# A hybrid encoder trunk on one core: modulations as products in column quarters, and written orders for the first stage and the units

## The chip, the cores and the metric

The kernel runs on one core of one Trainium2 chip. The core has a matrix engine (TensorE, PE in the rows; its weight loads are PEld), three engines for elementwise work (VectorE or DVE, ScalarE or ACT, GpSimd or POOL), and SyncE (SP), which here only issues transfers. Each engine runs its own list of instructions in order and waits on semaphores for the others. The metric is the device time of one execution in microseconds; lower is better.

## The reference, cut to what matters

Two residual layers of width 1024 over 512 tokens; layer 0 mixes by S5 and attention, layer 1 by a gated linear recurrence, each followed by an MLP with a squared ReLU. Shift, scale and gate of every part come from a conditioning vector `c`.

```python
mod = (c_act @ ada_w[layer] + ada_b[layer])            # 1024 x 6144
sh1, sc1, g1, sh2, sc2, g2 = jnp.split(mod, 6, axis=-1)
u = rms_norm(h, norm_w[layer, 0]) * (1.0 + sc1) + sh1
z = u @ hyb_w_in[e]                                     # columns: s5 | q | k | v
# s5, for each of two directions: abar = exp(lr*dt) * (cos, sin)(li*dt); b scaled by f(abar);
# complex linear scan over the 512 tokens; y += Re(h c); then gelu and a gated linear unit
# attention: rms norm of each head of q and k, rotary tables, softmax(q k / 8) v
mix = jnp.concatenate([y_s5, y_att], axis=-1) @ hyb_w_out[e]
h = h + g1 * mix
```

All is float32; the kernel multiplies large matrices as three products of rounded parts (`wh`, `wl` the rounded weight and its remainder; `acta`, `actb` the same of the activations).

## The kernel before

Only `hybrid` (L1113 to L1242), the first part of layer 0, is touched. It has four stretches.

*First stage.* x is loaded as eight tiles `h` of 128 features by 512 tokens. `rstd_bc` (L742) adds their squares (ACT squares into `nt`, DVE adds into `nacc`, L752) and spreads the reciprocal root. The modulation of features comes in four blocks of 512 columns (256 of shift, 256 of scale), each for two tiles: `ada_load` fetches the eight raw tiles of a block, `ada_block` (L708) adds them up on DVE, weighted by a column of `cact` (L715 a multiply, L717 seven multiply-adds of 128x512), and four products with `ones` (L719) fold the partitions. `norm_tile` then makes `acta` (ACT, L769) and `actb` (DVE, L770) of one tile, `wtile` casts its weights (`wh` on ACT, L512; `wl`, the remainder, L513, on POOL for the first three tiles and on DVE after), and TensorE adds 36 products for k and v (`psk`, 256 columns) and q (`psq`, 512), L599 to L601.

*Parameters.* `s5_params` (L164) makes the powers of abar, some hundred operations on 32 to 160 columns. It runs on POOL; the class `Tiny` splits the forms that POOL does in two. `s5_tables` (L290) makes sine tables on DVE and ACT. `s5_prep` (L328) forms the scaled b and c of one unit (`s5par` is fetched on ACT's queue; complex products `s5vr`, `s5vi`, `s5cv`, L341 to L345, on POOL but for one unit; ACT copies them to `s5c`, L356, and `s5bx`), transposes them, and `s5_lag` multiplies the lags on TensorE (L406) into `s5dc` on DVE (L415, L421).

*To the first unit.* `s5_in` makes the s5 columns of z in two halves (8 tiles each). `attn_kv` and `attn_q`: `head_ss` (L899) squares each head of 64 columns with an accumulator; q is rotated (`qr`), multiplied by its reciprocal root on POOL (L945), cast on ACT (L946) and the cast subtracted on POOL (L947).

*Units.* Eight units, for four groups in two directions (`for i in range(8)`). A unit makes phases (`s5_phase`, ACT), its states (`s5_states`: products L441 into `pb` and `p`, DVE multiplies L446 to L448, four scans L455 into `actb`), and the turn back (`s5_turn`: four POOL multiplies L466 to L469, two DVE additions L472 and L473, products L477). Beside them run attention steps (`step`): scores L967 and L968, maximum on DVE L970, exponential on ACT L972, transposes L980, products with v L989. `STEPS` gives their count before and after the next preparation: 23 of 35 calls in the units, the rest in `fill`. Gate (0, 2) is made by `ada_half`: 16 transfers on ACT's queue and 16 DVE operations (L668, L673), half of them each at the units in `FIN`.

A scheduler with its own costs sets each engine's order; the written code sets only the order on equal terms and the buffers. Behind the units come `fill` (the gated unit, the output products) and the boundary norm, then the MLP, layer 1 and its MLP.

Of the kernel before, what the change touches and what calls it, by code (L numbers as in the profile page):

```python
# [19 lines left out]
P = 128  # L20
# [5 lines left out]
STEPS = ((2, 2),) * 5 + ((2, 1),) + ((0, 0),) * 2  # L26
PREP_V = (2,)

EARLY, FIN = (0, 0, 2), (3, 4)
# [31 lines left out]


class Tiny:


    def __init__(self, kern, pool, eng):
        self.kern, self.pool, self.eng = kern, pool, eng
        self.tensor_scalar, self.tensor_tensor = eng.tensor_scalar, eng.tensor_tensor
        self.tensor_copy, self.memset = eng.tensor_copy, eng.memset

    def scalar_tensor_tensor(self, out, a, s, b, op0, op1):
        n = math.prod(out.shape[1:])
        t = self.kern.tl(self.pool, "tiny", [P, 160], bufs=2)[:, 0:n]
        if len(out.shape) == 3:
            t = t.rearrange("p (a b) -> p a b", b=out.shape[2])
        self.eng.tensor_scalar(t, a, s, None, op0=op0)  # L76
        self.eng.tensor_tensor(out, t, b, op=op1)


class Kern:  # L80
# [54 lines left out]
    def setup(self, cols, consts):  # L135
# [23 lines left out]
        self.sel = self.cp.tile([P, 32], F32, tag="sel", name="sel")  # L159
        self.glubh = self.cp.tile([P, 4], F32, tag="glubh", name="glubh")  # L160
# [3 lines left out]
    def s5_params(self, sp, tp):  # L164
        nc = self.nc
        V = D = Tiny(self, tp, nc.gpsimd)
# [6 lines left out]
        def pexp(x):  # L173
            n, r, p, o = t("n"), t("r"), t("p"), self.tl(tp, self.nm("pexp"), [P, W])
            V.tensor_scalar(n, x, 1.4426950408889634, MAGIC, op0=ALU.mult, op1=ALU.add)
            V.tensor_scalar(n, n, MAGIC, None, op0=ALU.subtract)
            V.scalar_tensor_tensor(r, n, -0.693359375, x, op0=ALU.mult, op1=ALU.add)
            V.scalar_tensor_tensor(r, n, 2.12194440e-4, r, op0=ALU.mult, op1=ALU.add)
            V.tensor_scalar(p, r, 1.9875691500e-4, None, op0=ALU.mult)
            for cf in (1.3981999507e-3, 8.3334519073e-3, 4.1665795894e-2, 1.6666665459e-1, 5.0000001201e-1, 1.0):  # L180
                V.scalar_tensor_tensor(p, p, cf, r, op0=ALU.add, op1=ALU.mult)
            V.tensor_scalar(p, p, 1.0, None, op0=ALU.add)
            V.tensor_scalar(n, n, -127.0, 128.0, op0=ALU.max, op1=ALU.min)
            e = t("e", dt=I32)
            V.tensor_scalar(e, n, 127.0, 8388608.0, op0=ALU.add, op1=ALU.mult)
            V.tensor_tensor(o, p, e.bitcast(F32), op=ALU.mult)
            return o
# [3 lines left out]
        dt = pexp(ldt)  # L191
# [11 lines left out]
        def reduce(a, n):  # L203

            D.tensor_scalar(n, a, 0.15915494309189535, MAGIC, op0=ALU.mult, op1=ALU.add)
            D.tensor_scalar(n, n, MAGIC, None, op0=ALU.subtract)
            for c in (c1, c2, c3):
                D.scalar_tensor_tensor(a, n, -c, a, op0=ALU.mult, op1=ALU.add)
            D.tensor_scalar(a, a, -pi, pi, op0=ALU.max, op1=ALU.min)

        def sincos(co, si, a, n):
            reduce(a, n)
            nc.vector.scalar_tensor_tensor(n, a, -1.0, a, op0=ALU.mult, op1=ALU.min)
            D.tensor_scalar(n, n, math.pi / 2, None, op0=ALU.add)
            nc.scalar.activation(si, a, AF.Sin)
            nc.scalar.activation(co, n, AF.Sin)

        reduce(r, t("rn"))
# [6 lines left out]
        for lo, ks in ((0, slice(0, 5)), (16, slice(4, None, -1))):  # L225
            D.tensor_tensor(ppi[:, lo:lo + 16], r[:, lo:lo + 16].unsqueeze(2).to_broadcast([P, 16, 5]),
                            kidx[:, ks].unsqueeze(1).to_broadcast([P, 16, 5]), op=ALU.mult)
        sincos(pr, ppi, ppi, npr)
        mag = pexp(x)
        V.memset(mt, 1.0)  # L230
        m = lambda k: ((mt[:, 0:16, k], slice(0, 16)), (mt[:, 16:32, 4 - k], slice(16, 32)))
        for o, h in m(1):
            nc.scalar.copy(o, mag[:, h])
        m2 = t("m2")
        V.tensor_tensor(m2, mag, mag, op=ALU.mult)
        for o, h in m(2):
            nc.scalar.copy(o, m2[:, h])
        for o, h in m(3):
            V.tensor_tensor(o, m2[:, h], mag[:, h], op=ALU.mult)
# [14 lines left out]
        nr, den, ta, fr, fi = t("nr"), t("den"), t("ta"), t("fr"), t("fi")  # L254
        V.tensor_scalar(nr, ar, 1.0, None, op0=ALU.subtract)
        V.tensor_tensor(den, lr, lr, op=ALU.mult)
        V.tensor_tensor(ta, li, li, op=ALU.mult)
        V.tensor_tensor(den, den, ta, op=ALU.add)
        nc.vector.reciprocal(den, den)
        V.tensor_tensor(fr, nr, lr, op=ALU.mult)  # L260
        V.tensor_tensor(ta, ai, li, op=ALU.mult)
        V.tensor_tensor(fr, fr, ta, op=ALU.add)
        V.tensor_tensor(fr, fr, den, op=ALU.mult)
        V.tensor_tensor(fi, ai, lr, op=ALU.mult)
        V.tensor_tensor(ta, nr, li, op=ALU.mult)
        V.tensor_tensor(fi, fi, ta, op=ALU.subtract)
# [5 lines left out]
        tb = self.tl(tp, "s5tb", [P, W, 4])  # L272
        for lo in (0, 16):
            sl = slice(lo, lo + 16)
            sv = slice(3, None, -1) if lo == 0 else slice(4, 0, -1)

            def b4(x):
                return x[:, sl].unsqueeze(2).to_broadcast([P, 16, 4])

            V.tensor_tensor(fpr[:, sl], pr[:, sl, sv], b4(fr), op=ALU.mult)  # L280
            V.tensor_tensor(tb[:, sl], npi[:, sl, sv], b4(fi), op=ALU.mult)
            V.tensor_tensor(fpr[:, sl], fpr[:, sl], tb[:, sl], op=ALU.add)
            V.tensor_tensor(fpi[:, sl], pr[:, sl, sv], b4(fi), op=ALU.mult)
            V.tensor_tensor(tb[:, sl], ppi[:, sl, sv], b4(fr), op=ALU.mult)
            V.tensor_tensor(fpi[:, sl], fpi[:, sl], tb[:, sl], op=ALU.add)
        nc.scalar.mul(nfpi, fpi, -1.0)
        V.tensor_scalar(r, r, 0.15915494309189535, None, op0=ALU.mult)
        self.s5 = dict(pr=pr, npr=npr, npi=npi, fpr=fpr, fpi=fpi, nfpi=nfpi, m4=m4, turns=r)

# [38 lines left out]
    def s5_prep(self, tp, pg, d, bc_dram, eng):  # L328

        nc, s5 = self.nc, self.s5  # L330
# [4 lines left out]
        nc.scalar.dma_start(par, bc_dram[d * 4 + pg].rearrange("p (a x c) -> p a x c", a=4, x=4))  # L335
# [17 lines left out]
        for src, dst in zip(cv, cs):  # L353
            for g in range(2):
                r = slice(g * 64, g * 64 + 64)
                A.copy(dst[r, :, g], src[r])  # L356

# [7 lines left out]
        sl0 = 3 if d == 0 else 0  # L365
        bx = []
        for j, src in enumerate((vr, vi)):
            t = self.tl(tp, f"s5bx{j}", [P, 4, 4, 16], bufs=1)
            A.copy(t, src[:, :, sl0].unsqueeze(2).to_broadcast([P, 4, 4, 16]))
            bx.append(t)  # L370
        self.s5u[(pg, d)] = bt, cs
        return bx, cs

    def s5_phase(self, sp, pg, d, eng):

# [1288 lines left out]
```

## Time and profile before

| | us |
|---|---|
| median of 3 runs (lowest to highest) | 1255.64 (1254.99 to 1257.53) |
| profiled execution, its own time | 1256.23 |
| its span, first to last instruction | 1254.4 |
| TensorE busy (share of the span) | 1161.8 (93%) |
| DVE busy | 804.5 (64%) |
| ACT busy | 532.3 (42%) |
| POOL busy | 240.4 (19%) |
| mean granted clock of TensorE | 0.959 |

Times in the rows are us from the start of the span; 1.8 us of the profiled execution's time lie outside it. Matmuls overlap in the rows, so a sum of their durations is more than the time they take. A float32 product (not rounded) shows as two records. A wait is put down to the releaser that came last.

### The profile page before, as it was taken

To read this page: it belongs to the slowest core of one execution; us is meant where nothing else is said; L and a number is where in the kernel's file an instruction comes from. 1 tells how busy PE (TensorE), PEld (TensorE's weight loads), DVE (VectorE), ACT (ScalarE), POOL (GpSimd) and SP (SyncE) were. 2 spreads that over 40 slices of the span, in tenths; PEclk is the share of its full clock that TensorE was granted. 3 is DMA by queue.
4 is the path that set the end of the run, shared out by engine and by line. 5 is a ranking of instruction groups with operands and counts; after the bars stand their busy time and mean duration, and the time that the engine had idled before them with its cause. 6 is when DMAs were issued, how large, how long until landed. Compare 5 with 4: busy or idle time off the path is not lost.

```text
span 1254.4 us, 16894 instructions
## 1 busy us (share of the span) xinstructions
PE 1161.8 (93%) x6456; PEld 983.0 (78%) x6456; DVE 804.5 (64%) x1182; ACT 532.3 (42%) x962; POOL 240.4 (19%) x346
## 2 busy tenths in 40 slices
PE   3678798889999999999999999789999999999997
PEld 2568577667998888888888988569988888888887
DVE  7548897988789875678433789995753332445243
ACT  3147577645452332134322449853543321334130
POOL 9996995410000000000000053000000000000000
PEclk9989697979999999999999999789999999999998
DMA  9411301065538765667332332112242223322311
GB/s 337 130 56 58 113 20 35 2 201 153 194 108 272 265 205 190 208 204 248 102 101 85 101 109 76 51 56 79 73 129 88 98 101 101 90 96 101 101 34 67
DMA packets 83856, 151.74 MB, mean 121 GB/s; under 512 B 5696, under 2 KB 30272, under 8 KB 83776
## 3 DMA queue, kind: packets, MB, share of 16 engines
q1 hardware_dynamic: 75712, 137.04, 33.6%
q10 hardware_dynamic: 8064, 13.64, 3.5%
q8 instruction: 50, 0.82, 0.3%
q14 instruction: 30, 0.25, 0.1%
HBM read 148.55 MB, written 2.10 MB: 120 GB/s over the span
## 4 chain that ended last, share of the span: by engine, by line
PE 71%; DVE 13%; POOL 8%; ACT 3%; issue 2%; DMA 1%; SPq 0%; ACTq 0%; DVEq 0%; POOLq 0%
PE ps L560 13%; PE ps L561 12%; PE ps L559 12%; PE px L559 8%; PE px L561 8%; PE px L560 8%; DVE wl L513 2%; POOL tiny L76 1%; DVE actb L455 1%; DMA wr<-wout 1%; PE py L477 1%; PE po L989 1%; DVE ti L1411 1%; DVE hs L1410 1%; DVE esum L970 1%
## 5 line engine op out<-in xcount | busy, mean ns | idle before, releaser
L513 DVE TENSOR_TENSOR wl<-wr,wh 128x1024 fp32r<-128x1024 f32 (+2 forms) x175 | 211.3, 1208 | 298.4 <-ACT wh L512 291.5
L512 ACT CAST wh<-wr 128x1024 fp32r<-128x1024 f32 (+2 forms) x170 | 173.6, 1022 | 436.5 <-PE ps L560 200.1
L560 PE MATMUL ps<-actb,wh 128*128 128x512 f32 (+1 forms) x512 | 181.3, 354 | 0.1
L559 PE MATMUL ps<-acta,wh 128*128 128x512 f32 (+1 forms) x328 | 116.8, 357 | 0.0
L561 PE MATMUL ps<-acta,wl 128*128 128x512 f32 (+1 forms) x328 | 116.1, 355 | 0.0
L559 PE MATMUL ps<-hid,wh 128*128 128x512 f32 x288 | 112.1, 389 | 0.0
L561 PE MATMUL ps<-hid,wl 128*128 128x512 f32 x288 | 112.0, 389 | 0.0
L560 PE MATMUL ps<-hid,wh 128*128 128x512 f32 x288 | 112.0, 389 | 0.0
L560 PEld LDWEIGHTS ps<-actb,wh 128*128 128x128 f32 x512 | 97.7, 191 | 13.5 <-DVE actb L849 0.3
L559 PE MATMUL px<-hid,wh 128*128 128x512 f32 (+1 forms) x288 | 98.9, 343 | 0.0
L560 PE MATMUL px<-hid,wh 128*128 128x512 f32 (+1 forms) x288 | 98.5, 342 | 0.0
L561 PE MATMUL px<-hid,wl 128*128 128x512 f32 (+1 forms) x288 | 98.5, 342 | 0.0
L560 PE MATMUL px<-actb,wh 128*128 128x512 f32 (+1 forms) x224 | 85.5, 382 | 0.0
L641 DVE SCALAR_TENSOR_TENSOR acc<-wr,cact,acc 128x1024 f32<-128x1024 f32 x49 | 62.8, 1282 | 16.8 <-DMA wr<-ada_w 16.3
L559 PEld LDWEIGHTS ps<-acta,wh 128*128 128x128 f32 x328 | 63.0, 192 | 8.5
L561 PEld LDWEIGHTS ps<-acta,wl 128*128 128x128 f32 x328 | 62.7, 191 | 8.5
L1338 POOL MEMSET xp<- 128x2 f32 x8 | 0.7, 98 | 348.0 <-PE px L561 343.7
L559 PE MATMUL ps<-actc,wh 128*128 128x512 f32 (+1 forms) x184 | 65.1, 354 | 0.0
L561 PE MATMUL ps<-actc,wl 128*128 128x512 f32 (+1 forms) x184 | 64.8, 352 | 0.0
L559 PEld LDWEIGHTS ps<-hid,wh 128*128 128x128 f32 x288 | 54.1, 188 | 11.2
L560 PEld LDWEIGHTS ps<-hid,wh 128*128 128x128 f32 x288 | 54.1, 188 | 11.2
L561 PEld LDWEIGHTS ps<-hid,wl 128*128 128x128 f32 x288 | 54.0, 188 | 11.2
(504 smaller groups left out, 2709.8 us busy)
## 6 DMA issues: line engine op xcount, KB each, us to landing
wr<-w SPq DMA_DIRECT2D x128, 512.0 KB, 3.7
wr<-ada_w SPq DMA_DIRECT2D x56, 512.0 KB, 4.4
wr<-wout SPq DMA_DIRECT2D x16, 512.0 KB, 3.6
araw<-ada_w ACTq DMA_DIRECT2D x32, 256.0 KB, 3.1
wr<-win SPq DMA_DIRECT2D x16, 512.0 KB, 3.8
acta<-ada_w SPq DMA_DIRECT2D x16, 256.0 KB, 5.5
actb<-ada_w SPq DMA_DIRECT2D x16, 256.0 KB, 5.5
nt<-ada_w ACTq DMA_DIRECT2D x16, 256.0 KB, 2.9
```

The lines of the kernel that those rows point to most:

```text
L76: self.eng.tensor_scalar(t, a, s, None, op0=op0)
L455: self.scan = V.tensor_tensor_scan(*z, 0.0, op0=ALU.mult, op1=ALU.add)
L477: mm(p4[:, x], h[:, o:o + P], c[:, x], start=(d == 0 and x == 0 and i == 0), stop=False, skip_group_check=True)
L512: nc.scalar.copy(hi, src)
L513: (lo_eng or nc.vector).tensor_tensor(lo, src, hi.bitcast(F32), op=ALU.subtract)
L559: mm(out, wh, xh, start=first and a == a0 and lead(o), stop=False, skip_group_check=True)
L560: mm(out, wh, xl, start=False, stop=False, skip_group_check=True)
L561: mm(out, wl, xh, start=False, stop=last and a == a0 + kk - 1, skip_group_check=True)
L641: nc.vector.scalar_tensor_tensor(acc, raw, self.ca[:, k:k + 1], acc, op0=ALU.mult, op1=ALU.add)
L970: nc.vector.reduce_max(nb, s, axis=AX.X, negate=True)
L989: self.nc.tensor.matmul(po[h2 * 64:h2 * 64 + 64, t * 128:(t + 1) * 128], self.vp[:, kb, p // 2], pts[h2][:, kb * 128:(kb + 1) * 128], star ...
L1410: V.tensor_tensor_scan(hs, a[:, 0], ti[:, 0], 0.0, op0=ALU.mult, op1=ALU.add)
```

## The change

The change rewrites `hybrid` up to the end of its units; `fill`, the MLPs and layer 1 are left as they are.

- **Modulations.** A block is eight products on TensorE: the column of `cact`, repeated to 32 columns, is the stationary side, the raw 512 columns the moving one, and product k writes the partitions of quarter k mod 4. ACT copies the sum out, and four small products with `sel` fold it. Gate (0, 2) goes the same way in four pieces of 256 columns (`ada_quarter`), loaded on SP and finished in units 1 to 4. All raw tiles of the first stage have buffers of their own.
- **Orders.** The new function `front` is the first stage, with the order of PE, DVE and ACT as written; in the units the order of PE is as written (`manual`). Squares go through five buffers in turn; the weights have four raw buffers in place of three, and every remainder `wl` is made on DVE.
- **Parameters.** `s5_params` runs on DVE, with the exponential and the angle as two chains that alternate, in parts that `front` calls between norm tiles; the rotary tables go to DVE. `s5_prep` is cut in parts, its transfer on SP, and belongs to the unit three later.
- **Attention.** `head_ss` is one square over all heads and a DVE sum. q isn't multiplied by its reciprocal root; the exponential takes it as a scale, with the negative maximum scaled by a small ACT operation. The units hold 2, then 7 x 3, then 2 steps: 25.

```diff
-STEPS = ((2, 2),) * 5 + ((2, 1),) + ((0, 0),) * 2
+STEPS = ((0, 0, 2),) + ((1, 1, 1),) * 7
+LAST = 2
 PREP_V = (2,)
-EARLY, FIN = (0, 0, 2), (3, 4)
+FIN = (1, 2, 3, 4)
...
-class Tiny:
...
-        V = D = Tiny(self, tp, nc.gpsimd)
+        V = D = nc.vector
...
+        def together(*chains):
+            chains = list(chains)
+            while chains:
+                chains = [c for c in chains if next(c, c) is not c]
...
+        together(angles(), pexp(x, mag))
...
-        nc.scalar.dma_start(par, bc_dram[d * 4 + pg].rearrange("p (a x c) -> p a x c", a=4, x=4))
+        nc.sync.dma_start(par, bc_dram[d * 4 + pg].rearrange("p (a x c) -> p a x c", a=4, x=4))
+        yield
...
+            yield vr, vi
...
-    def ada_block(self, pool, raws, cb, ps):
-        nc = self.nc
-        acc = self.tl(pool, "pexp", [P, 512], bufs=3)
+    def ada_products(self, raws, ps):
         for k in range(8):
-            raw = raws[k].rearrange("p q n -> p (q n)")
-            if k == 0:
-                nc.vector.tensor_scalar(acc, raw, self.ca[:, 0:1], None, op0=ALU.mult)
-            else:
-                nc.vector.scalar_tensor_tensor(acc, raw, self.ca[:, k:k + 1], acc, op0=ALU.mult, op1=ALU.add)
-        for i in range(4):
-            nc.tensor.matmul(ps[:, i:i + 1], acc[:, i * P:(i + 1) * P], self.ones, start=True, stop=True)
+            o = k % 4 * 32
+            self.nc.tensor.matmul(ps[o:o + 32, 0:raws[k].shape[1]], self.ca[:, k:k + 1].to_broadcast([P, 32]), raws[k],
+                                  start=k < 4, stop=k >= 4, skip_group_check=True)
+    def ada_fold(self, acc, ps, n=4):
+        for i in range(n):
+            self.nc.tensor.matmul(ps[:, i:i + 1], acc[:, i * P:(i + 1) * P], self.sel[:, 0:1], start=True, stop=True)
...
+    def ada_quarter(self, aw, l, q, n, raws, acc, tag):
+        nc = self.nc
+        c0 = q * 1024 + n * 256
+        for j, raw in enumerate(raws):
+            nc.sync.dma_start(raw, aw[l, j * 256:(j + 1) * 256, c0:c0 + 256].rearrange("(a p) n -> p a n", p=P))
+        def finish():
+            ps = self.psum(tag)
+            self.ada_products([raws[k // 2][:, k % 2] for k in range(8)], ps)
+            s = acc()
+            nc.scalar.copy(s, ps[:, 0:256])
+            self.ada_fold(s, ps, 2)
...
+            sq = self.tl(pool, "pexp", [P, 512], bufs=3) if k % 2 else self.tl(self.sp, "nt", [P, 512], bufs=2)
...
-        sq = self.tl(hp, "hsq", [P, 64], bufs=2)
-        for h in range(nh):
-            self.nc.scalar.activation(sq, ps[:, h * 64:(h + 1) * 64], AF.Square, accum_out=dst[:, h:h + 1])
+        sq = self.tl(hp, "tmp", [P, 512], bufs=3)[:, 0:nh * 64]
+        self.nc.scalar.activation(sq, ps, AF.Square)
+        self.nc.vector.reduce_sum(dst, sq.rearrange("p (h d) -> p h d", h=nh), axis=AX.X)
...
-        rq = self.rsqrt(self.sp, ss.rearrange("p t h -> p (t h)"), 32, 64.0, "rq")
-        nc.vector.tensor_scalar(rq, rq, 0.125, None, op0=ALU.mult)
-        for t in range(4):
-            o = self.qr[t]
-            nc.gpsimd.tensor_tensor(o[:, :, 0], o[:, :, 0], rq[:, t * 8:t * 8 + 8].unsqueeze(2).to_broadcast([P, 8, 64]), op=ALU.mult)
+        self.rq = self.rsqrt(self.sp, ss.rearrange("p t h -> p (t h)"), 32, 64.0, "rq")
+        nc.vector.tensor_scalar(self.rq, self.rq, 0.125, None, op0=ALU.mult)
...
+        r = self.rq[:, t * 8 + h:t * 8 + h + 1]
+        nc.scalar.activation(nb, nb, AF.Identity, scale=r)
+        self.exp = nc.scalar.activation(p, s, AF.Exp, bias=nb, scale=r, accum_out=self.esum[:, h, t:t + 1])
...
+        for cb in range(4):
+            k = 2 * cb
+            u += self.norm_pair(x[k:k + 2], xbc, m)
+            if cb == 0:
+                split(c)
+            if cb == 1:
+                raws.append(self.ada_load(aw, 3, hp, qp))
+                next(params)
+            if cb < 3:
+                if cb:
+                    wl += [ld(k + 2), ld(k + 3)]
+                split(wl[k + 2][0]())
+            products(k, kv, 256, 512)
+            if cb < 3:
+                pb = self.psum("p5")
+                block(cb + 1, pb)
+                s = evacuate(pb)
+            products(k, psq, 512, 0)
+            if cb < 3:
+                c = wl[k + 3][0]()
+                self.ada_fold(s, pb)
+            if cb < 2:
+                next(params)
+            products(k + 1, kv, 256, 512)
+            if cb < 3:
+                m = self.ada_mod(cb + 1, pb[:, 0:4])
+                split(c)
+            products(k + 1, psq, 512, 0)
+        self.fr = u, psq, psk
...
+        def unit(i):
             pg, d = i // 2, i % 2
-            if i == 0:
-                uts.append(self.s5_ut(lp, sz[0]))
-            if d == 1 and pg < 3:
-                uts.append(self.s5_ut(lp, sz[pg + 1]))
+            pr = prep(i + 3) if i < 5 else iter(())
+            next(pr, None)
+            next(pr, None)
             if d == 0:
                 gts.append(self.tl(self.hp, "h", [P, 512], bufs=9))
             e = self.s5_phase(lp, pg, d, self.POST[i][0])
             if i == 3:
                 self.s5_tables(sp, 1)
-            v = self.s5_states(lp, pg, d, *e, uts[pg])
-            if d == 0:
-                pys.append(self.psum("py"))
-            self.s5_turn(pg, d, e[0], *v, self.POST[i][1], pys[pg])
-            for _ in range(STEPS[i][0]):
-                self.step(att)
-            if i + UNITS - 3 < 8:
-                prep(i + UNITS - 3)
-                if i + UNITS - 3 == 7:
-                    pctx.close()
-                    self.weights(rctx, 3, 2, side="right")
+            st = self.s5_states(lp, pg, d, *e, uts[pg])
+            next(st)
+            steps(STEPS[i][0])
+            v = next(st)
+            next(st, None)
+            turns.append(self.s5_turn(pg, d, e[0], *v, self.POST[i][1]))
+            steps(STEPS[i][1])
+            so = iter(())
+            if i:
+                outputs(i - 1)
+                if d == 0:
+                    so = out(pg - 1)
+                    next(so)
+            next(pr, None)
+            if d == 0 and pg < 3:
+                uts.append(self.s5_ut(lp, sz[pg + 1]))
+            steps(STEPS[i][2])
+            next(so, None)
+            next(pr, None)
+            if i == 4:
+                next(pr, None)
+                pctx.close()
+                self.weights(rctx, 3, 2, side="right")
             if i in FIN:
                 fins.pop(0)()
-            for _ in range(STEPS[i][1]):
-                self.step(att)
-            if d == 0 and pg > 0:
-                out(pg - 1)
-        out(3)
-        for f in fins:
-            f()
+                if i < FIN[-1]:
+                    fins.append(quarter(i))
...
+            for i in range(8):
+                unit(i)
+            steps(LAST)
```

TensorE at the start of the first stage, before (`p_95`, `p_106` are the folds of blocks 0 and 1, `nry` the reciprocal root, `ps_391` to `ps_396` q, k and v):

```order
L755 MATMUL ps_371<-ones,nacc_348 128x1 x4
L719 MATMUL p_95_397<-ones,pexp_398 128x1 x4
L759 MATMUL ps_385<-consts_sb,nry_377 128x128 x4
L599 MATMUL ps_395<-wh_448,acta_455 128x256
L599 MATMUL ps_396<-wh_448,acta_455 128x256
L599 MATMUL ps_391<-wh_448,acta_455 128x512
L599 MATMUL ps_392<-wh_448,acta_455 128x512
L599 MATMUL ps_393<-wh_448,acta_455 128x512
L599 MATMUL ps_394<-wh_448,acta_455 128x512
L719 MATMUL p_106_430<-ones,pexp_431 128x1 x4
L600 MATMUL ps_395<-wl_449,acta_455 128x256
```

After (`p_54` holds block 0, `p_58` the spread root, `ps_304` the first of k and v):

```order
L752 MATMUL p_54_262<-actb_159,cact 32x512
L752 MATMUL p_54_262<-acta_161,cact 32x512
L752 MATMUL p_54_262<-actb_163,cact 32x512
L1193 MATMUL p_58_280<-consts_sb,nry_272 128x128 x4
L758 MATMUL p_54_262<-sel,pexp_289 128x1 x4
L630 MATMUL ps_304<-wh_285,acta_308 128x256
L631 MATMUL ps_304<-wl_287,acta_308 128x256
L632 MATMUL ps_304<-wh_285,actb_309 128x256
L630 MATMUL ps_304<-wh_285,acta_308 128x256
```

Six first products with `wh` stood ahead of the fold of block 1 and of all products with `wl`; now products of block 0 (eight in a row, the last three shown) come ahead of the root, and each tile's three products stand together.

DVE at the seam of units 6 and 7, before (`actb_2632` and `actb_2667` belong to unit 6's turn, `pb_594`, `p_596` and `s5e_2698` to unit 7):

```order
L455 SCALAR_TENSOR_TENSOR actb_2633<-s5m4t_2623,p_583_2651 128x255
L447 TENSOR_TENSOR pb_594_2712<-s5e_2698,pb_594_2712 128x512
L448 TENSOR_TENSOR pb_594_2712<-pb_594_2712,s5m_2721 128x512
L1042 TENSOR_TENSOR tmp_2395<-po_1966,tmp_2395 128x512
L455 SCALAR_TENSOR_TENSOR actb_2708<-s5m4t_2699,pb_594_2712 128x255
L455 SCALAR_TENSOR_TENSOR actb_2709<-s5m4t_2699,pb_594_2712 128x255
L446 TENSOR_TENSOR s5m_2736<-s5e_2698,p_596_2727 128x512
L472 TENSOR_TENSOR actb_2667<-actb_2667,actb_2668 128x511
L513 TENSOR_TENSOR acta_2399<-tmp_2395,acta_2398 128x512
L447 TENSOR_TENSOR p_596_2727<-s5e_2698,p_596_2727 128x512
L970 TENSOR_REDUCE esum_1198<-pa_572_2608 128x1
L473 TENSOR_TENSOR actb_2632<-actb_2632,actb_2633 128x511
```

After, the seam of units 5 and 6 (`actb_2355`, `actb_2403` are unit 5's, `pb_519` and `s5e_2458` unit 6's):

```order
L463 SCALAR_TENSOR_TENSOR actb_2356<-s5m4t_2346,p_501_2388 128x255
L1094 RECIPROCAL rsum_2547<-esum_1128 128x8
L1096 TENSOR_SCALAR tmp_2549<-rsum_2547 128x512
L479 TENSOR_TENSOR actb_2403<-actb_2403,actb_2404 128x511
L1028 TENSOR_REDUCE esum_1128<-pa_510_2443 128x1
L480 TENSOR_TENSOR actb_2355<-actb_2355,actb_2356 128x511
L454 TENSOR_TENSOR s5m_2481<-s5e_2458,pb_519_2472 128x512
L455 TENSOR_TENSOR pb_519_2472<-s5e_2458,pb_519_2472 128x512
L1028 TENSOR_REDUCE esum_1128<-pa_521_2487 128x1
L456 TENSOR_TENSOR pb_519_2472<-pb_519_2472,s5m_2481 128x512
```

Before, several multiplies and scans of the next unit stood ahead of the turn's additions (L472, L473); now the two additions (L479, L480) of a unit stand ahead of the first multiply (L454) of the next, with one reduction between them.

## Rows read from the trace of the kernel before

**Rows 1.** Table of stretches: busy us (instructions) of each engine, granted clock, DMA share, GB/s.

```profile
42.00:87.00 45.00, 38.87 (x203) 34.24 (x203) 24.02 (x35) 12.09 (x28) 41.77 (x70) 0.89 0.39 120
87.00:134.00 47.00, 38.07 (x328) 34.17 (x327) 33.95 (x70) 37.50 (x154) 36.70 (x43) 0.94 0.23 67
134.00:256.00 122.00, 105.14 (x827) 81.50 (x826) 109.89 (x173) 79.90 (x175) 86.54 (x120) 0.82 0.14 43
256.00:353.00 97.00, 93.01 (x632) 78.78 (x631) 77.36 (x136) 46.63 (x87) 2.60 (x3) 0.94 0.56 181
353.00:1255.00 902.00, 877.07 (x4436) 745.52 (x4435) 531.08 (x723) 342.72 (x501) 34.71 (x44) 0.98 0.38 122
```

**Rows 2.** Waits of TensorE, 0 to 135 us: waiter, releaser, total us, times, longest.

```profile
PE ps L600 <- POOL wl L513: 11.1, 1, 11.1
PE ps L599 <- ACT acta L769: 8.0, 2, 5.7
PE p L719 <- DVE pexp L717: 4.0, 1, 4.0
```

**Rows 3.** Timeline of TensorE around its first products: start, us, what, [idle before].

```profile
27.38 2.50 PE L599 MATMUL ps<-wh,acta 128*128 128x256 f32 x6 [2.36 <-ACT acta L769]
...
42.47 0.58 PE L600 MATMUL ps<-wl,acta 128*128 128x256 f32 x1 [11.09 <-POOL wl L513]
```

**Rows 4.** Chain of waits, the pieces ahead of the first unit: start, us, what.

```profile
101.83 2.26 ACT hsq L902 x21
...
117.94 4.64 POOL qr L945 x4
...
126.53 4.62 POOL qr L947 x3
131.52 1.93 PE p L406 x16
```

**Rows 5.** Timeline of DVE: start of unit 0 and end of the last turn.

```profile
133.94 0.68 DVE L446 TENSOR_TENSOR s5m<-s5e,pb 128x512 f32<-128x512 f32 x1
...
256.03 0.68 DVE L473 TENSOR_TENSOR actb<-actb,actb 128x511 f32<-128x511 f32 x1
```

**Rows 6.** Groups of DVE, 0 to 134 us: what, count, busy us, mean ns, idle before.

```profile
L717 DVE SCALAR_TENSOR_TENSOR pexp<-actb,cact,pexp 128x512 f32<-128x512 f32 x16 | 11.8, 740 | 0.1
...
L717 DVE SCALAR_TENSOR_TENSOR pexp<-acta,cact,pexp 128x512 f32<-128x512 f32 x12 | 9.0, 754 | 0.2
```

**Rows 7.** Chain of waits: products of a turn in float32, 128 columns each.

```profile
215.64 1.78 PE py L477 x16
```

**Rows 8.** Waits of DVE, 0 to 50 us.

```profile
DVE nacc L752 <- ACT nt L751: 2.4, 1, 2.4
```

**Rows 9.** Groups of ACT, 90 to 135 us: the heads' squares.

```profile
L902 ACT ACTIVATE hsq<-ps 128x64 f32<-128x64 f32 x40 | 8.7, 258 | 0.1
L902 ACT ACTIVATION_READ_ACCUMULATOR hsq<-ps 128x1 f32 x40 | 8.4, 240 | 0.0
```

**Rows 10.** Groups of DVE, 134 to 260 us: reductions, gate, additions of the turns.

```profile
L970 DVE TENSOR_REDUCE esum<-pa 128x1 f32<-128x512 f32 x24 | 16.2, 678 | 7.0 <-PE pa L968 7.0
...
L673 DVE SCALAR_TENSOR_TENSOR h<-nt,cact,h 128x512 f32<-128x512 f32 x9 | 9.7, 1073 | 2.2 <-DMA nt<-ada_w 2.2
L472 DVE TENSOR_TENSOR actb<-actb,actb 128x511 f32<-128x511 f32 x8 | 7.1, 884 | 0.0
```

**Rows 11.** Groups of POOL, 134 to 260 us: two of the four multiplies of a turn.

```profile
L469 POOL TENSOR_TENSOR actb<-s5e,actb 128x511 f32<-128x511 f32 x8 | 11.3, 1418 | 0.0
...
L466 POOL TENSOR_TENSOR actb<-s5e,actb 128x511 f32<-128x511 f32 x8 | 9.4, 1178 | 30.9 <-DVE actb L455 30.9
```

**Rows 12.** Groups of TensorE, 256 to 353 us: one score product of a step.

```profile
L967 PE MATMUL pa<-kth,q 128*128 128x512 f32 x9 | 5.0, 551 | 0.6 <-ACT pexp L972 0.6
```

More of the change, by code (lines that the diff above doesn't have):

```diff
@@ L364, in s5_prep @@
         A.copy(bt.rearrange("p i x m -> p (i x m)"), ps)
[L365 to L370, printed above, removed]
         self.s5u[(pg, d)] = bt, cs
-        return bx, cs
+        yield
+        self.s5_lag(tp, pg, (bx, cs), d)
+        yield
     def s5_phase(self, sp, pg, d, eng):
@@ L516, in wraw, with wload, cast, rest @@
         return self.tl(self.wp, "wr", [P, self.WC], bufs=self.WR)
+    def wload(self, src):
+        raw = self.wraw()[:, 0:src.shape[1]]
+        self.nc.sync.dma_start(raw, src)
+        def cast():
+            hi = self.tl(self.wp, "wh", [P, self.WC], F32R, bufs=self.WH)[:, 0:src.shape[1]]
+            self.nc.scalar.copy(hi, raw)
+            return hi
+        def rest(hi):
+            lo = self.tl(self.wp, "wl", [P, self.WC], F32R, bufs=self.WH)[:, 0:src.shape[1]]
+            self.nc.vector.tensor_tensor(lo, raw, hi.bitcast(F32), op=ALU.subtract)
+            return lo
+        return cast, rest
     def wtile(self, src, pool=None):
@@ L1160, in hybrid @@
-        self.lo_eng = None
+        ld = lambda k: self.wload(win[k * P:(k + 1) * P, 512:1280])
+        raws = [self.ada_load(aw, 0, hp, qp)]
+        wl = [ld(0), ld(1)]
+        raws.append(self.ada_load(aw, 1, hp, qp))
+        wl += [ld(2), ld(3)]
+        pre = [prep(i) for i in range(2)]
+        for pr in pre:
+            next(pr)
+        raws.append(self.ada_load(aw, 2, hp, qp))
+        params = self.s5_params(sp, tp)
+        E = mybir.EngineType
+        with self.tc.manual_schedule(engines={E.PE, E.DVE, E.Activation}):
+            self.front(x, win, aw, raws, wl, ld, params, hp, qp)
@@ L1188, in hybrid, with steps, outputs @@
         out = lambda pg: self.s5_out(lp, pg, uts[pg], pys[pg], gts[pg])
-        for i in range(8):
+        def steps(n):
+            for _ in range(n):
+                self.step(att)
+        def outputs(i):
+            if i % 2 == 0:
+                pys.append(self.psum("py"))
+            turns[i](pys[i // 2])
+        def unit(i):
             pg, d = i // 2, i % 2
-            if i == 0:
-                uts.append(self.s5_ut(lp, sz[0]))
-            if d == 1 and pg < 3:
-                uts.append(self.s5_ut(lp, sz[pg + 1]))
+            pr = prep(i + 3) if i < 5 else iter(())
+            next(pr, None)
+            next(pr, None)
             if d == 0:
```

303 lines of the change are left out of this document (170 added, 133 removed).

## The prediction

> **What bounds the kernel now.** I read the table of stretches first. From 353 us to the end TensorE is busy 877 of 902 us and the change touches nothing there; between 256 and 353 us it is busy 93 of 97 [rows 1]. What can shrink lies before 256 us, where TensorE stands still for much of the time: 38.9 us of work in the 45 us from 42 to 87, 38.1 in the 47 from 87 to 134, and 105 in the 122 of the eight units [rows 1], though in the units it is not the engine that sets the pace; there DVE is busy 109.9 of 122 us [rows 1]. So: first stage bound by its inputs, then a chain of small engines, then units bound by DVE and its exchange with POOL, then TensorE.
>
> The waits of TensorE name the inputs of the first stage: 11.1 us for one weight remainder `wl` that POOL makes, 8.0 us for `acta` (ACT's normed x) [rows 2]. In the timeline the first six products run at 27.38, and the rest begin only at 42.47 [rows 3]. The chain of waits shows what leads from there to the first unit: a run of ACT's squares and accumulator reads for the heads (21 of them in 2.26 us), then POOL's multiply of q (4.64 us) and its subtract (4.62 for three), then lag products of TensorE at 131.5 [rows 4]. The first DVE operation of unit 0 stands at 133.94, the last of unit 7's turn (L473) at 256.03 [rows 5]; 353 us is fixed by TensorE's work behind that. What moves 256 moves the end, one to one.
>
> **First stage: the products leave DVE.** Before, four blocks cost DVE 28 multiply-adds (11.8 + 9.0 us [rows 6]) and four multiplies, most of it ahead of or between the tiles that TensorE wants. After, TensorE does 8 products of 512 columns per block, four at a time in quarters of the columns. No product of that shape is in the trace. The nearest is L477: 16 records in 1.78 us, two records to a product of 128 columns, so 0.22 us each [rows 7]; 512 columns are four times that, 0.89. One after another a block is 8 x 0.89 = 7.1 us, four at a time 1.8. I take 1.8, because the four quarters write disjoint partitions and nothing else in the code orders them; 7.1 stays as the other bound. Nothing is gained below 1.8. Blocks 1 to 3 stand on TensorE's path, 3 x 1.8 = 5.4 us; block 0 is done before the norm's sum can be.
> The records at L477 neither show nor exclude that quarters run together. The Trainium skill, page "TensorEngine Tiling (Array Packing)", section "Theoretical Speedup", gives up to 4 times for 32 columns, and the page "TensorE: Matmul & The Clock Gate", section "Measured speedup vs the span model", measured 2.38 for three such tiles; scaled to four that is about 3.2, an estimate, and a block 2.2 us instead of 1.8, 1.3 us more in all. The first page's section "Key Properties" speaks against the change: a change of tiling mode drains the engine, and each block stands between products of full width. No row here shows that drain.
>
> **First stage: written order and parameters on DVE.** The remainder that POOL made late (11.1 us of wait [rows 2]) goes to DVE, right behind the norm. The first products lose the wait for block 0's sum, 4.0 us [rows 2], and the wait of the squares for a buffer, 2.4 [rows 8]; the first 20 parameter operations, now on DVE ahead of the rsqrt, give some 2 back. So they begin at 27.4 - 4.0 - 2.4 + 2 = 23 us and go on without the stop, against 42.47 [rows 3]. TensorE's products from 42 to 87 are 38.9 us of work [rows 1]; with the 5.4 of the blocks and the six products done early (about 2.5 [rows 3]) they would end at 23 + 38.9 + 2.5 + 5.4 = 70. They won't run without a wait. The parameters, some 100 small operations, stand in DVE's order between the norm tiles: row by row I find TensorE waiting about 7 us for the remainder of the fifth tile behind them, and about 4 us for ACT, whose copies for the preparation (they wait for POOL) stand ahead of its casts. That gives about 80, against 87 before. Bounds: 70 with neither wait, 90 if the blocks are serial as well (10 more).
>
> **From there to the first unit.** `head_ss` loses 40 squares and 40 accumulator reads on ACT, 8.7 + 8.4 us [rows 9], for 8 squares and 8 DVE sums. q's multiply by rq on POOL, 4.64 us on the chain, is gone [rows 4]; the rsqrt chain for q no longer stands ahead of ACT's cast and POOL's subtract. Then q is ready beside the second half of `s5_in`. What is late next is the preparation: POOL's products for it, ACT's copies `s5c`, lag products, unit 0. POOL has lost the parameters (it is busy 41.8 of 45 us from 42 to 87 [rows 1]), so they end near 107, and the first DVE operation of unit 0 I place at 120 instead of 133.94: **14 us**. With bounds from the first stage: 6 to 22.
>
> **The units.** DVE loses the gate's multiply-adds (9.7 us and 2.2 of waits for their transfers between 134 and 260) and gains two more reductions at 0.68 [rows 10] and five small operations for folds and modulations; its work falls from 109.9 to about 101.5 us [rows 1]. The gate's 32 products of 256 columns on TensorE fall into its idle time. ACT gets one tiny operation per step for rq, about 0.2 us by its accumulator reads of 0.24 [rows 9], 25 of them: 5 to 6 us on an engine that works 80 of 122 us [rows 1]; I count nothing, and the whole 6 if ACT becomes late.
> Against that stands DVE's new order: the second addition of the turn (L480) now stands ahead of the first multiply of the next unit, where L473 stood behind several of its operations. It needs POOL's four multiplies, which follow the last scan. They cost 1.18 to 1.42 each [rows 11], 5.2 together; DVE has the first addition (0.88 [rows 10]) and one or two reductions to do meanwhile, so it idles up to 2.7 us per unit, 8 x 2.7 = 22. Before, its idle time was 122 - 109.9 = 12. The units then take between 101.5 + 5 (DVE packed) and 101.5 + 22 = 123.5. I take 115 to 116, a little above the middle, since POOL also carries the preparations ahead of the first turns: **6 us** less than 122, and 15 to -2 as bounds.
>
> **Behind the units.** 25 attention steps instead of 23 are done by then, so 10 instead of 12 remain where TensorE is full. A step's two score products cost 0.55 [rows 12] and about as much again, its transposes and products with v come on top, partly side by side; I take 1.5 a step: **3 us**. Nothing and 5 are the bounds.
>
> **Sum.** The profiled run took 1256.23 us, 0.6 above the median of the runs. 1256.2 - 14 - 6 - 3 = 1233; against the median 1232.6. Forecast 1233, its own range 1225 to 1241.
>
> **Rivals.**
> *Packed:* the front waits for neither parameters nor ACT (22 instead of 14) and DVE runs its units with little idle time (15): 1256 - 22 - 15 - 3 = 1216, down to 1207 if the clock in the units also rises (granted 0.82 there, 0.98 later [rows 1]). For it: POOL's parameter load is gone. Against: orders are fixed by hand, and an engine that waits holds all that stands behind.
> *Lockstep:* L480 costs its full 2.7 in each unit, and the first turns wait behind POOL's preparations as well: units 124 to 126, gain 14 - 3 + 3 = 14, 1242; with the early waits a little longer up to 1252.
> *Quarters one after another:* 3 x 5.3 = 16 us more on TensorE in the first stage, of which 6 fall into its waits there: 10 lost, 1243. A block's products at 0.89 us each would show it.
> *Slower:* the written order on TensorE in the units. If a unit's steps don't overlap with its scans, a unit is states and phase, scans and multiplies 7.3, POOL 5.2, addition, turn products 1.8, then three steps each held by a reduction and an exponential, about 21 us; 120 + 8 x 21 = 288 against 256, or 1285. It decides from (256 + 3 - 120) / 8 = 17.4 us per unit. Against: the steps stand in three places of the unit, between products of other sorts.
> *No change:* the entry gains 14 and the units give it back, the point between; little room.
>
> **How the numbers follow.** Forecast 0.45, packed 0.20, lockstep 0.16, serial quarters 0.05, no change 0.03, slower 0.11. A measurement of this kernel tells about 0.2% (2.5 us) from no change. Faster 0.86, same 0.03, slower 0.11. The range reaches from packed's 1207 to 1257, just past no change; beyond it lie most of the slower case and a little of the packed one.
>
> **What would show it.** Right: first products at about 23 us with no stop behind the first six; `ada` products of a block in 1.8 to 2.2 us; q's products done by 76 to 84; first multiply of unit 0 at 117 to 123; DVE idle ahead of L480 for some 2 us per unit; last addition of unit 7 at 233 to 240. Wrong: a long DVE stretch of parameters with TensorE idle for over 10 us; TensorE waiting for its own order between states and steps; units over 17 us; ACT above nine tenths busy in the units.

## The result and the profile after

The changed kernel took 1269.88 us (median of 4 runs, 1268.80 to 1274.09) against 1256.14: 1.0115 times the kernel before, interval 1.009 to 1.014. It is slower by some 14 us where 23 us of gain were forecast. Its profiled execution was the longest of the four, 1274.09 us, with a span of 1272.3 (before: 1256.23 and 1254.4), so the stretches below stand up to 4 us above an ordinary execution.

The table of stretches of the changed kernel, cut at its own seams (columns as in [rows 1]): products of q, k and v; the way to unit 0; the eight units; the work behind them up to the norm.

```profile
24.00:85.00 61.00, 48.69 (x268) 37.81 (x269) 40.74 (x111) 24.88 (x52) 22.08 (x24) 0.86 0.41 141
85.00:127.00 42.00, 33.32 (x314) 31.25 (x314) 26.66 (x57) 27.50 (x73) 33.89 (x46) 0.91 0.16 49
127.00:274.00 147.00, 114.03 (x908) 88.14 (x904) 104.52 (x163) 86.80 (x195) 72.84 (x102) 0.80 0.13 40
274.00:369.00 95.00, 88.96 (x623) 75.92 (x622) 75.75 (x132) 48.61 (x93) 1.69 (x2) 0.97 0.54 180
```

Unit 0's first multiply and the last addition of unit 7's turn, in the timeline of DVE (before: [rows 5]):

```profile
127.02 0.69 DVE L454 TENSOR_TENSOR s5m<-s5e,pb 128x512 f32<-128x512 f32 x1 [10.15 <-PE pb L449]
...
272.86 1.09 DVE L480 TENSOR_TENSOR actb<-actb,actb 128x511 f32<-128x511 f32 x1
```

So unit 0 starts at 127.0 instead of 133.9, but the units last 146.9 us instead of 122.8. The 18 us between the two spans are -6.9 in front, +24.2 in the units, -0.8 behind them (to the first product of the norm's sum at 368.95, before 352.48) and 1.4 in all that follows. In the units TensorE's granted clock averaged 0.80, TensorE was busy 114.0 and DVE 104.5 of 147 us: no engine there is full.

Waits of TensorE in the units (waiter, releaser, total us, times, longest):

```profile
PE pa L1025 <- ACT pexp L1032: 17.1, 6, 8.4
PE po L1049 <- ACT pts L1042: 6.0, 9, 2.9
PE p L758 <- ACT nacc L771: 4.1, 4, 1.7
```

Waits of DVE in the same stretch:

```profile
DVE s5m L454 <- PE pb L449: 14.9, 6, 10.2
DVE esum L1028 <- PE pa L1026: 12.7, 8, 2.8
...
DVE actb L480 <- POOL actb L477: 4.5, 4, 1.8
```

TensorE stands still for 33 of the 147 us, half of it for ACT's exponential, and next for the copies of the transposes; DVE waits for scores and states from TensorE, but only 4.5 us for the second half of POOL's turn and 4.6 for the first (10.2 of the 14.9 us for states lie ahead of unit 0). In the kernel before no wait of DVE of this kind was longer than 7.0 in total ([rows 10], L970).

The first stage went about as the forecast had it: in the timeline of TensorE the first product starts at 23.9, block 2 takes 1.92 us, and the stop is ahead of the fifth tile:

```profile
23.92 0.58 PE L630 MATMUL ps<-wh,acta 128*128 128x256 f32 x1 [2.06 <-ACT acta L827]
...
38.52 1.92 PE L752 MATMUL p<-raw,cact 128*32 128x512 f32 x16
...
55.66 0.58 PE L630 MATMUL ps<-wh,acta 128*128 128x256 f32 x1 [7.19 <-ACT acta L827]
```

### The profile page after: what moved, and what is told of

Read it like the earlier page. It is cut to its first block, busy times and chain, and to the rows that moved or that the text cites. A ratio compares the mean times of both kernels' runs of the same rounds, so it can differ in the third digit from the quotient of the medians.

```text
span 1272.3 us, 17003 instructions
## 1 busy us (share of the span) xinstructions
PE 1170.8 (92%) x6584; PEld 984.4 (77%) x6584; DVE 795.3 (63%) x1230; ACT 541.7 (43%) x929; POOL 171.2 (13%) x232
## 4 chain that ended last, share of the span: by engine, by line
PE 76%; DVE 12%; ACT 6%; POOL 3%; issue 2%; DMA 0%; DVEq 0%; ACTq 0%; POOLq 0%
PE ps L591 12%; PE ps L592 12%; PE ps L590 12%; PE px L590 8%; PE px L592 8%; PE px L591 8%; DVE wl L527 2%; PE po L1049 1%; POOL s5ptmp L348 1%; PE py L487 1%; DVE ti L1552 1%; PE pt L1040 1%; DVE hs L1551 1%; PE p L752 1%; PE pn L859 1%
## 5 line engine op out<-in xcount | busy, mean ns | idle before, releaser
L527 DVE TENSOR_TENSOR wl<-wr,wh 128x1024 fp32r<-128x1024 f32 (+1 forms) x170 | 206.9, 1219 | 277.5 <-ACT wh L526 271.1
L526 ACT CAST wh<-wr 128x1024 fp32r<-128x1024 f32 (+1 forms) x162 | 166.5, 1030 | 425.2 <-PE ps L591 200.2
L591 PEld LDWEIGHTS px<-hid,wh 128*128 128x128 f32 x288 | 54.6, 190 | 6.3
```

What stands on the lines that cost most here:

```text
L526: nc.scalar.copy(hi, src)
L527: (lo_eng or nc.vector).tensor_tensor(lo, src, hi.bitcast(F32), op=ALU.subtract)
L591: mm(out, wh, xl, start=False, stop=False, skip_group_check=True)
```

## The experiments

"Start" is unit 0's first multiply, "units" reach from there to the end of the last addition, "behind" from there to the norm's first product, all in us of one profiled execution, which can lie some 4 us off the median (changed: 1274.09 against 1269.88; e7's lies 9 off). Ratios are to the kernel before, run on the same chip beside each.

| kernel | start | units | behind | ratio (95% interval) |
|---|---|---|---|---|
| before | 133.9 | 122.8 | 95.8 | 1 |
| changed | 127.0 | 146.9 | 95.0 | 1.0115 (1.009 to 1.014) |
| e1_sched | 128.0 | 115.2 | 95.0 | 0.9890 (0.9868 to 0.9912) |
| e2_units_before | 125.5 | 119.0 | 99.6 | 0.9948 (0.9933 to 0.9962) |
| e3_steps18 | 124.8 | 132.9 | 117.3 | 1.0202 (1.0182 to 1.0221) |
| e4_q_scaled | 121.7 | 143.9 | 95.5 | 1.0083 (1.0066 to 1.0100) |
| e5_states_ahead | 124.9 | 141.2 | 95.2 | 1.0112 (1.0081 to 1.0142) |
| e7_prep12_dve | 127.7 | 117.3 | 94.6 | 0.9846 (0.9830 to 0.9863) |
| e8_params_pool | 139.3 | 114.5 | 95.5 | 0.9986 (0.9972 to 1.0001) |
| e9_ada_dve | 146.0 | 114.1 | 96.3 | 1.0024 (1.0012 to 1.0035) |
| e10_full_width | 144.2 | 114.5 | 93.8 | 0.9996 (0.9986 to 1.0005) |
| e11_front_sched | 114.1 | 110.9 | 94.1 | 0.9737 (0.9723 to 0.9752) |
| e13_sched_steps18 | 127.3 | 113.8 | 121.0 | one run, 1267.56 us |
| e14_prep3_later | 124.1 | 113.6 | 91.2 | 0.9813 (0.9798 to 0.9827) |
| e15_front_pe | 117.2 | 113.0 | 92.5 | 0.9788 (0.9766 to 0.9810) |
| e16_front_dve | 122.8 | 111.1 | 96.0 | 0.9830 (0.9809 to 0.9851) |
| e17_front_act | 116.8 | 110.4 | 95.0 | 0.9771 (0.9751 to 0.9790) |
| e18_best | 109.2 | 114.5 | 94.7 | 0.9754 (0.9725 to 0.9783) |

**The order of the units.** e1_sched takes TensorE's written order away:

```diff
-        with self.manual():
+        if True:
             for _ in prep(2):
```

> The changed kernel, but in the units TensorE's order is the scheduler's again instead of the written one. Theory W (the written order holds TensorE behind ACT and DVE): the units fall from 147 us back to about 122 or less, the time from 1269.9 to 1235-1248. Theory A (each attention step is longer because ACT scales the maximum first): units within 4 us of 147, 1266-1272. Theory P (TensorE simply has more to do in the units: gate products and two more steps): 1266-1272 as well.

Measured 1245.17 us, ratio 0.9890; the units fell to 115.2 us, 32 less, with the same operations (by the ratios the whole is 28 us shorter). Its stretches and its waits of TensorE in the units:

```profile
24.00:85.00 61.00, 49.39 (x272) 36.95 (x272) 40.73 (x113) 25.02 (x55) 22.08 (x24) 0.87 0.42 143
...
128.00:243.00 115.00, 100.94 (x921) 77.90 (x918) 103.76 (x162) 85.86 (x199) 72.85 (x101) 0.93 0.17 52
```

```profile
PE py L487 <- DVE actb L479: 4.9, 3, 3.7
PE po L1049 <- ACT pts L1042: 3.5, 3, 2.6
PE pb L449 <- DVE actb L463: 2.2, 2, 1.2
PE pa L1025 <- ACT pexp L1032: 1.1, 3, 0.6
```

The wait for the exponential is down to 1.1 us from 17.1, and the granted clock up to 0.93 from 0.80. Of the 32 us, 19 are waits of TensorE that are gone (33 to 14) and 13 are products that take less time (busy 114.0 to 100.9). Theory W is shown: the order alone turned the gain into a loss.

e2_units_before puts the loop of the kernel before (its steps, its preparation two units ahead, gate in `ada_half`) on the new front:

> The new first stage, parameters, head squares and scaled exponential, but the units as in the kernel before (its loop, its 23 steps, scheduler's order, preparation two units ahead, gate on DVE in two halves). W and P: the entry's 7 us remain, units 122 again: 1247-1251. A: the steps are still longer, units 130-147: 1258-1270. The entry itself should be as in the changed kernel: first multiply of unit 0 at 126-129.

Measured 1251.81, ratio 0.9948, just above the range W gave: the new front, with the head squares and the scaled exponential, is worth some 6 us under the old loop. Against e1_sched the units are 4 us longer and the work behind them nearly 5.

**What in the written order costs.** e3_steps18 and e13_sched_steps18 set `STEPS` to `((0, 0, 2),) + ((1, 0, 1),) * 7`, in the written and in the scheduler's order:

> The changed kernel with 18 attention steps in the units instead of 25 (the middle one of each unit left to the work behind). P: a step costs TensorE the same in either place, about 2.7 us; units 147 - 19 = 128, tail longer by the same, time within 3 us of 1269.9. W: the middle step's waits go with it, 7 x 3 to 4 us off the units against 7 x 1.5 to 2.7 more in the tail: 1255-1266. A: like W, since each step is long.

> The units' order left to the scheduler, with 18 steps in the units instead of 25; read for the length of the units alone (114.8 us with 25 steps; in the written order 146.9 with 25 and 132.3 with 18, so 2.1 us a step). Theory I (a written step isn't hidden, a scheduled one is): 111 to 115, under 0.6 us a step. Theory P (TensorE's work bounds the units either way): 98 to 102, about 2 us a step.

Seven steps fewer shorten the written units by 14.0 us, 2.0 us each, and the scheduled ones by 1.4, 0.2 each; each figure rests on one pair of traces. Scheduled, a step fits beside the rest; written, it is added to it. The time of e3 went against all three theories, 1283.88: behind the units seven more steps cost 22 to 26 us, over 3 each, where they had been priced at 1.5 to 2.7.

e5_states_ahead keeps the written order and calls phase and first states of the next unit (`head(i + 1)`) ahead of the last step:

```diff
...
+            if i < 7:
+                heads[i + 1] = head(i + 1)
             steps(STEPS[i][2])
...
```

> The changed kernel (14 us above the kernel before) with TensorE's written order kept, but phase and first states of the next unit moved ahead of the last step, the lag products and the gate piece of the unit. Theory S (what costs is that a unit's first states stand behind everything of the unit before, so DVE waits for them, 18.6 us in the trace): units from 147 to 128-133, time from 14 above to within 4 of the kernel before. Theory I (what costs is the order inside the attention steps, scores and transposes waiting for ACT): the time stays 9 to 14 above.

Measured 1270.74, ratio 1.0112, no change. Waits of TensorE, then of DVE, in its units:

```profile
PE pa L1025 <- ACT pexp L1032: 22.0, 8, 8.1
PE p L758 <- ACT nacc L771: 5.5, 4, 1.9
```

```profile
DVE s5m L454 <- PE p L449: 9.5, 5, 3.9
...
DVE s5m L454 <- PE pb L449: 2.7, 3, 1.9
```

DVE waits 12 us for states, where it waited 8 in the changed kernel, and TensorE longer than before for the exponential: theory S falls. Its 18.6 us had also counted the 10.2 ahead of unit 0. A place for the states alone doesn't mend the order; which single order would was not searched further.

e4_q_scaled gives back q's multiply (POOL, ahead of the cast) and drops the scale and the small ACT operation:

> The changed kernel, but q is multiplied by its reciprocal root on POOL again and the exponential has no scale and no small ACT operation ahead of it. A: 25 steps shorter by 0.3-0.5 us of a chain that TensorE waits on: 1258-1264. W: the time moves by under 3 us, since what stands in front of TensorE's waits is its own order; first multiply of unit 0 within 2 us of 127. P: under 3 us.

Measured 1268.50, ratio 1.0083; units 143.9. The small operation isn't the cause; some 3 us of the units and 5 of the start could be its or chance, since six kernels with the changed front (changed, e1, e2, e3, e5, e13) start anywhere between 124.8 and 128.0.

**The parts of the first stage**, each on e1_sched. e8_params_pool puts the parameters back on POOL (`V = D = Tiny(self, tp, nc.gpsimd)`); e9_ada_dve sums the blocks on DVE:

```diff
-        block = lambda cb, ps: self.ada_products(raws[cb], ps)
...
+            nc.vector.tensor_scalar(s, raws[cb][0], self.ca[:, 0:1], None, op0=ALU.mult)
+            for k in range(1, 8):
+                nc.vector.scalar_tensor_tensor(s, raws[cb][k], self.ca[:, k:k + 1], s, op0=ALU.mult, op1=ALU.add)
...
```

e10_full_width keeps TensorE but not the quarters (`ps[:, ...]`, the column of `cact` repeated to 128 columns):

> The units' order left to the scheduler, and the parameters back on POOL, in the form of the kernel before (two operations where POOL lacks the form), in the new chains and parts. If their place on DVE gave what the entry gained: first multiply of unit 0 at 136 to 142 instead of 127, time from 13.8 below to 5 below up to 3 above. If their place was hidden: 12 to 16 below.

> The units' order left to the scheduler, and the first stage's four blocks summed by DVE again (eight operations of 512 columns each, folded with ones), in the same written order. If the column quarters carry the first stage's gain: each block holds DVE 5.7 us ahead of the next norm, three of them on the path, 10 to 17 us later at unit 0, time 4 below to 4 above. If DVE has room there (it waits about 16 us between 40 and 87): 8 to 13 below.

> The units' order left to the scheduler (13.8 us below the kernel before), and the modulation products no longer in quarters: the column of cact is repeated to all 128 columns, eight products of full width one after another, folded with one column of the identity. This prices the quarters by themselves. If the quarters run side by side (a block was 1.85 us in the trace of the changed kernel) a block should take 6.8 to 7.1 us here; three blocks on the path are 15 us more, less what falls into TensorE's waits: 5 to 10 us later at unit 0, time 4 to 9 below the kernel before. If the waits hide it all: 12 to 15 below.

Starts of 139.3, 146.0 and 144.2 against 128.0: with the written order of the first stage, parameters on DVE are worth 11 us, products on TensorE 18, the quarters among them 16. In the chain of waits of e10_full_width the third block reads

```profile
49.10 6.87 PE p L751 x16
```

against 1.92: 3.6 times as long. It isn't three blocks that count but four: block 0 holds the first product of k and v, too, which starts at 29.1 instead of 23.6. Together the four take 32.7 us against 11.7 in e1_sched (granted clock 0.56 and 0.64 over two of its blocks, 0.83 and 0.84 over two of e10_full_width's). That is 21 more, and the start is 16 later: some 5 us fell into waits.

**The order of the first stage.** e11_front_sched leaves it to the scheduler as well, on e1_sched:

```diff
-        with self.tc.manual_schedule(engines={E.PE, E.DVE, E.Activation}):
+        if True:
             self.front(x, win, aw, raws, wl, ld, params, hp, qp)
```

> The units' order left to the scheduler, and the first stage too: front is traced as it stands, but the order of PE, DVE and ACT is the scheduler's. If the written order gives the first stage its gain: products end 5 to 10 us later, time 4 to 9 below the kernel before. If the order is worth nothing there and the rest (products on TensorE, parameters on DVE) carries it: 12 to 16 below.

Measured 1225.03, ratio 0.9737: both expectations were wrong, the written order costs here too. Stretches of e11_front_sched (to its last product of q, and the units), and its waits of TensorE between 16 and 90 us:

```profile
24.00:71.00 47.00, 45.75 (x279) 36.03 (x280) 29.96 (x77) 23.62 (x55) 19.41 (x24) 1.00 0.55 185
...
114.00:225.00 111.00, 94.40 (x897) 73.39 (x892) 99.65 (x161) 83.08 (x191) 71.62 (x102) 0.96 0.16 50
```

```profile
PE p L1193 <- DVE nry L802: 2.3, 1, 2.3
PE ps L630 <- ACT acta L827: 0.8, 1, 0.8
```

The first product starts at 29.0, five us later than in the changed kernel, but from there TensorE hardly waits, its granted clock is 1.00, and the last product of q ends at 70.4 instead of 84.7. The scheduler puts the first parameters on DVE ahead of and between the additions of the squares (3.7 to 13.6, written 13.9 to 17.3), and the sine table at 16.4 to 23.1, where the written order has it at 49.7 to 61.2, around the norm tiles of the stop. The early table holds the last DVE operation of the root back to 24.2, so the first product comes late; in return it no longer stands among the norm tiles of the stop. That this alone ends the stop isn't shown.

e15, e16 and e17 keep the written order on one engine (`engines={E.PE}`, `{E.DVE}`, `{E.Activation}`):

> Units by the scheduler; in the first stage TensorE's order alone is the written one, DVE and ACT are the scheduler's. With all three written unit 0 starts at 128 and the time is 13.8 below the kernel before, with none at 114 and 33 below. If DVE's order (parameters and sine tables between the norm tiles) holds the stage: start 114 to 118, 28 to 33 below. If TensorE's own order does (k and v, then q, each tile complete before the next): start 122 to 128, 14 to 22 below.

> As above, with DVE's order alone as written. If DVE's order holds the stage: start 122 to 128, 14 to 22 below the kernel before. If TensorE's or ACT's does: 114 to 118, 28 to 33 below.

> As above, with ACT's order alone as written. If ACT's order (casts of weights and normed tiles in program order) holds the stage: start 122 to 128, 14 to 22 below the kernel before. If DVE's or TensorE's does: 114 to 118, 28 to 33 below.

Starts of 117.2, 122.8 and 116.8 against 114.1: DVE's order costs 8.7 us, TensorE's 3.1 and ACT's 2.7, in sum 14.5, where all three cost 13.9. Each is one trace; e1, e7 and e13, which share the written first stage and the scheduled units, start within 0.7 us of each other.

**The copies for unit 3.** In e1_sched's timeline of ACT the copies `s5c` of a later unit wait for POOL ahead of the copies of the s5 columns, for which unit 0 waits:

```profile
114.53 1.87 ACT L361 COPY s5c<-s5cv 64x320 f32<-64x320 f32 x4 [4.41 <-POOL s5cv L350]
116.42 1.45 ACT L648 COPY h<-ps 128x128 f32<-128x128 f32 x8
```

e7_prep12_dve moves unit 1's complex products to DVE (`PREP_V = (1, 2)`); e14_prep3_later holds these copies back, on ACT alone, behind the copy `s5ut` that unit 0 needs (`self.utc`):

```diff
-            next(pr, None)
+            if i:
+                next(pr, None)
+            else:
+                with self.tc.issue_after(self.utc.ins):
+                    next(pr, None)
```

> The units' order left to the scheduler (that run was 13.8 us below the kernel before), and in addition the complex products of unit 1's preparation on DVE instead of POOL. If POOL's preparations set the first unit's start (its last products of the preparations end at 115, unit 0 starts at 127): the start comes 4 to 7 us sooner and the time is 17 to 21 below. If the s5 columns and ACT's copies set it: within 2 of 13.8 below.

> The units' order left to the scheduler, and ACT's copies for the preparation of unit 3 (they wait until 114.5 for POOL, and ACT's copies of the second half of the s5 columns stand behind them) held behind the copy that unit 0 needs. If those copies set the start: first multiply of unit 0 at 121 to 124 instead of 128, time 17 to 21 below the kernel before. If the s5 products on TensorE or the s5 table set it: start at 127 to 128, 12 to 16 below.

e7: start 127.7, unchanged, so POOL's products for unit 1 did not set it, though its ratio is 0.9846; its runs spread from 1233.93 to 1247.05, the profiled one being the slowest, and its gain is unexplained. e14: start 124.1, ratio 0.9813; the copies cost 4 us of the start. The rest of the 10 us is 2 in the units and 4 in the work behind them (91.2), for which I have no cause. e18_best joins e11 and e14:

> Scheduler's order in the first stage and in the units, and ACT's copies for unit 3 held behind the copy that unit 0 needs. If the two are separate causes (14 us and 4 us): start of unit 0 at 110, time 40 to 44 below the kernel before. If the earlier products already took what the copies held: start 113 to 115, 31 to 35 below.

Start 109.2, 5 us sooner: the causes are separate. But its units take 114.5 instead of 110.9 and the time is 1225.47, ratio 0.9754, 32 us below the kernel before and not 40 to 44: the same as e11 within the intervals. Why the units gave the gain back stays open. These two are the fastest measured, some 2.5% below the kernel before.

## Why the prediction was wrong

- **What bounds the kernel.** Right: all that moved lies ahead of the norm; behind it the time is the same within 1.4 us.
- **Products in quarters.** Right: 1.92 us a block (1.8 forecast, 7.1 the other bound; full width gave 6.87), though 3.3 in e1_sched's block 1, at a granted clock of 0.56. The rival of serial quarters is out. Its price of 10 us was too low because block 0 counts: it wasn't "done before the norm's sum can be" but ran behind it (15.8 to 19.4, with the root's input ready at 18.4), and at full width it was in the path. Of the 21 us, 5 were hidden and 16 lost. The Trainium skill, page "TensorE: Matmul & The Clock Gate", section "Measured speedup vs the span model", gave 2.38 for three tiles, from which 2.2 us a block was estimated; four measured 3.6 and the measurement decides. The drain that the Trainium skill, page "TensorEngine Tiling (Array Packing)", section "Key Properties", names can show here as no more than 0.13 us on the way in, by which the first product of block 1 stood off the usual spacing (27.14 behind 26.80, at a spacing of 0.21), and 0.09 on the way out (29.07 behind 28.55, at 0.43).
- **Written order of the first stage.** Start at 23 (23.9), wait for the fifth tile about 7 (7.2, though it ended with the normed x and not with the remainder), wait behind ACT's copies about 4 (3.0, ahead of the seventh tile), end about 80 (84.7). The waits were read off the order rightly, but they were taken as the price of moving the parameters to DVE. They were the price of the order: with the scheduler's the same operations end at 70. That this is also the bound that the forecast called "neither wait" is luck: they start at 29, not 23, and take 41 us at a granted clock of 1.00, not the forecast's 47, most of it read off at 0.89.
- **To the first unit.** 14 us forecast, 6.9 measured. Mis-sized by POOL's products for unit 3, which ended at 115 and not near 107, with ACT's copies behind them (e14, 4 us), and by the later end of the products.
- **The units.** The failing step. It put TensorE in the units down as not setting the pace, took DVE's and POOL's exchange for the limit, and gave 6 us of gain. That exchange was over-priced (L479 and L480 waited 9 us in all, where 14 were taken and 22 was the bound). What the runs showed in its place is TensorE as the engine that sets the pace, through its order: it waited 33 us in the units, and e1_sched, with that order given up, took 115.2 us for them. That this is the forecast's own figure is luck: no wait of L479 or L480 for POOL was left in it. The cost lay in the written order, which stood among the rivals as *Slower* at 0.11, with its point of decision at 17.4 us per unit; measured were 18.4. Its mechanism, steps not hidden beside the scans, is what e3 and e13 show; only its 21 us per unit were too many. The argument against it, that steps stand in three places of the unit, was no evidence: an in-order engine with a wait ahead of it has the rest of the unit behind that wait, wherever the step stands.
- **Behind the units.** 3 us for two steps, 0.8 measured between the two kernels, which differ in more than the steps. e2, with the 23 steps of before, took 4.6 more than e1 with 25, and seven fewer steps cost over 3 us each. So the 0.8 doesn't show that two steps are nearly free; their price there stays open.

## What to carry to other kernels

An order written by hand for several engines has to be priced wait by wait: on each engine, what stands behind the instruction that waits, and whether the wait's length depends on an engine that waits in turn. Here all the other edits together (products on TensorE, parameters on DVE, the attention's and the preparation's) were worth 33 us with the orders left to the scheduler (e11), and the two written orders took some 46 back; taking the orders away one at a time was the cheapest way to see both. An engine that looks slack by busy time can still set the pace if its order is fixed.

## What was not expected of the hardware

The granted clock went with the gaps: over the units it averaged 0.80 in the written order and 0.93 in the scheduler's, and over the products of q, k and v 0.86 with the stops and 1.00 without. The same products of 256 columns stood 0.21 us apart behind the stop that ended at 55.7 (granted clock 0.50 from 55.6 to 60.7, the lower level) and 0.12 without one (32.9 to 34.1, granted 1.00), so a stop costs more than its own length.
